# A smaller scratch for dynamic transfers, one more weight page and one more 4 KB buffer, in a two-layer mixer and expert network

## The chip, the cores and the metric

The kernel runs on one core of one Trainium2 chip, in one launch. The metric is the device time of that core in microseconds (us). Of the kernel before there are three timed runs: 2033.0, 2022.24 and 2030.6 us, with a median of 2030.6 us.

## What is computed

The reference is a network of two layers on two sequences of 256 tokens of width 1024, the context and the latent tokens, in float32. Cut to what matters here:

```python
for l in range(2):
    p_lat = dot(x * (1 + sc1) + sh1, w_in[l])            # w_in: 1024 x 3536
    p_ctx = dot(ctx * (1 + mod_c[1]) + mod_c[0], w_in[l])
    y_ctx, y_lat = token_mixers(p_ctx, p_lat, ...)       # attention, RWKV, mLSTM
    x = layer_norm(alpha * x + g1 * dot(y_lat, w_out[l]))
    h2 = x * (1 + sc2) + sh2                             # the same for ctx in layer 0
    f = hierarchical_moe(h2, ...)                        # 32 experts, 2 a token
    x = layer_norm(alpha * x + g2 * f)
```

An expert is `dot(silu(dot(h, w_gate)) * dot(h, w_up), w_down)` with three matrices of 1024 x 512 (or 512 x 1024) in float32, 2 MB each. All 32 experts of a layer get tokens, so each layer reads 192 MB of expert weights.

## The kernel before, in words

**Stages.** A layer has a mixer stage (projections, the three mixers, output projection, norm, router logits) and an expert stage. By the trace, the mixer stage of layer 0 runs from 0 to about 535 us, the experts of layer 0 to about 1075, the mixer stage of layer 1 to about 1510, and the experts of layer 1 with the last norm to the end.

**Pages.** Weights come into a pool named `ring` (line 221) of `NR` = 8 pages of 8 KB a partition, 1 MB each; `rg` (line 272) hands one out. Half an expert matrix fills a page. The same pages also hold the chunks of `w_in`, the modulation weights `w_mod`, `w_out`, the split input of the projections and some intermediates of the mixers. A second pool `hp` (line 239) has `NH` = 12 buffers of 4 KB; `h` and `hr` hand them out, for projected queries and keys, rows spread over the partitions, gathered tokens of the experts (`xe`) and their outputs (`yh`, `yl`).

**Order.** Nearly all loads are issued from SP's queue, one after the other; a load waits there until its page has been let go by its last reader, and everything behind it on SP waits too. The framework sorts the instructions of each engine ahead of time, by priorities (the table `CHOICES['pr']`) and by when it thinks that buffers come free, so the number of buffers enters that order. In the expert stage the matmuls alone are held in the order of the program (`self.pin`, line 1768).

**Expert stage.** `PLAN` (line 37) lists, for each layer, items of one, two, three or four experts, which go through 128 slots of tokens together. `experts` (line 1628) makes the steps of an item: in `first` the tokens go through gate and up, in `second` through down; `moe` (line 1723) weaves the steps of one item with those of the next. `first` goes over the eight row blocks of a matrix and, in each, over all experts of the item: an item of four experts holds four pages at a time and lets go of them together, one of two experts two.

```python
1646:             for (xe, so, runs), ps in zip(blocks, pgu[kind]):
1647:                 for c, m, r in runs:
1648:                     self.mm(ps[c:c + m, :], xe[half][:, j, so + c:so + c + m], wt[r][j], half + j == 0, half + j == 4)
```

`wpart` (line 1698) issues a load; line 1709 is the load into a page. Which expert comes at which rank is known only after the router (`etab`, read by SP). Experts 31 (and 30 in layer 1) are fixed, and their pages are loaded ahead of it (`ahead`, line 1915): in layer 0 four parts into pages and two into 4 KB buffers, in layer 1 seven into pages and the rest into other buffers.

**Scratch.** `Bacc` (line 2012) sets up the program. It reserves, unless told otherwise, 16 KB of each partition as a scratch for dynamic transfers. Sixteen transfers are issued from POOL (the profile's queue q0).

Of the kernel before, what the change touches and what calls it, by code (L numbers as in the profile page):

```python
# [144 lines left out]
        'tks': None,  # L145
        'pr': {'rw_mid': -200}}]}
CFG = dict(CHOICES)
NR, NH, NW, NQ = 8, 12, 15, 8
PB, PC, PE_ = 4, 2, 2
_NP = 69  # L150
_C = {}
# [1868 lines left out]
```

## Time and profile before

| what | value |
|---|---|
| median of three runs | 2030.6 us (2022.24 to 2033.0) |
| the profiled execution's own time | 2033.04 us |
| its span | 2031.2 us |
| mean granted TensorE clock | 0.949 of full speed |
| TensorE (PE) busy | 1800.4 us, 89% of the span |
| VectorE (DVE) / ScalarE (ACT) / GpSimd (POOL) busy | 47% / 25% / 13% |
| read from memory | 523.44 MB, 261 GB/s over the span |

The profile is of one execution. PE is TensorE's matmuls, SPq is the queue of SyncE, from which loads are issued. A view of waits lists who waited, at which line and on which tile, for whom. A view of stretches lists what each engine did between two times, the granted clock and how busy the sixteen transfer engines were.

### The profile page before, as it was taken

What the parts mean: (1) busy time and instruction counts of PE and PEld (TensorE: products, weight loads), DVE (VectorE), ACT (ScalarE), POOL (GpSimd) and SP (SyncE); (2) the same over time, 40 slices, a digit from 0 to 9 for tenths busy, and PEclk for the clock granted to TensorE, in tenths of its full rate; (3) what the DMA queues carried; (4) which work ended last, traced back from release to release, by engine and by line L of the source; (5) the groups of instructions that cost most, each with busy time, mean ns of one, the idle gap of its engine ahead of it and who ended that gap; (6) DMA issues with size and microseconds to landing.
All of it is one profiled execution on the core that took longest, in us unless ns stands there. A gap on an engine that the chain in (4) does not pass through costs nothing. (4 is left out here: it accounts for less than half of the span.)

```text
span 2031.2 us, 29550 instructions
## 1 busy us (share of the span) xinstructions
PE 1800.4 (89%) x11375; PEld 912.1 (45%) x11375; DVE 958.3 (47%) x2133; ACT 508.8 (25%) x1073; POOL 273.5 (13%) x204
## 2 busy tenths in 40 slices
PE   6999999799998899889996899997999988988884
PEld 2777875245533233324434677773453222323221
DVE  2686655567633334334446687744762222222223
ACT  1663413444110010001014654314521010100001
POOL 0000010034311112111221010010220001001001
PEclk9988999999999999999998899988899999999997
DMA  8432335733779998999992233347748979999995
GB/s 282 141 82 58 89 62 217 244 145 104 285 284 382 409 384 327 407 394 396 386 413 87 88 89 95 67 114 251 290 177 350 388 288 415 417 416 409 417 418 227
DMA packets 194224, 532.93 MB, mean 262 GB/s; under 512 B 77824, under 2 KB 108448, under 8 KB 156576
## 3 DMA queue, kind: packets, MB, share of 16 engines
q1 hardware_dynamic: 191936, 526.33, 68.9%
q0 software_dynamic: 992, 2.53, 0.4%
q8 instruction: 92, 1.51, 0.3%
q10 hardware_dynamic: 1152, 2.13, 0.3%
q14 instruction: 52, 0.43, 0.1%
HBM read 523.44 MB, written 7.50 MB: 261 GB/s over the span
## 5 line engine op out<-in xcount | busy, mean ns | idle before, releaser
L283 PE MATMUL ps<-rg,xe 128*32 128x512 f32 (+2 forms) x2280 | 478.0, 614 | 47.3 <-DMA rg<-in_exp_w_up_dram 27.7
L283 PE MATMUL pe<-rg,HT 128*32 128x512 f32 (+2 forms) x1120 | 236.0, 658 | 55.5 <-DMA rg<-in_exp_w_down_dram 44.4
L283 PE MATMUL ps<-rg,wh 128*128 128x512 f32 (+2 forms) x1056 | 260.0, 390 | 5.0 <-ACT wh L473 2.7
L283 PEld LDWEIGHTS ps<-rg,xe 128*32 128x32 f32 (+2 forms) x2280 | 107.8, 123 | 282.6 <-issue 180.3
L1686 DVE TENSOR_TENSOR sc<-pw,bc 128x512 f32<-128x512 f32 x164 | 112.1, 690 | 220.3 <-PE pw L283 218.9
L283 PEld LDWEIGHTS ps<-rg,wh 128*128 128x128 f32 (+1 forms) x1056 | 182.4, 195 | 53.8 <-issue 13.3
L1687 POOL TENSOR_TENSOR acc<-acc,sc 128x512 f32<-128x512 f32 x82 | 106.0, 1293 | 587.5 <-DVE sc L1686 587.5
L283 PEld LDWEIGHTS pe<-rg,HT 128*32 128x32 f32 (+2 forms) x1120 | 66.0, 131 | 220.6 <-issue 122.0
L1676 DVE SCALAR_TENSOR_TENSOR yl<-pe,sw,yh 128x512 fp32r<-128x512 f32 x54 | 40.4, 750 | 237.4 <-ACT yh L1675 234.6
L1675 ACT ACTIVATE yh<-pe,sw 128x512 fp32r<-128x512 f32 x54 | 36.9, 687 | 311.1 <-PE pe L283 288.2
L1652 ACT ACTIVATE H<-ps 128x512 f32<-128x512 f32 x27 | 16.1, 598 | 313.1 <-DVE acc L1687 302.9
L283 PE MATMUL pw<-oh,hi 128*128 128x256 f32 x336 | 90.7, 306 | 1.5 <-DVE oh L1590 1.5
L283 PE MATMUL pw<-yh,ot 128*128 128x512 f32 x164 | 84.2, 513 | 1.8 <-DVE sc L1686 1.5
L283 PE MATMUL pw<-oh,lo 128*128 128x256 f32 x336 | 83.8, 285 | 0.0
L283 PEld LDWEIGHTS pw<-yh,ot 128*128 128x128 f32 x164 | 30.7, 187 | 116.4 <-DVE sc L1686 57.6
L283 PEld LDWEIGHTS pw<-oh,hi 128*128 128x128 f32 x336 | 64.7, 192 | 39.8 <-issue 24.1
L283 PE MATMUL ps<-wh,rg 128*128 128x256 f32 x384 | 77.7, 294 | 0.0
L1622 POOL TENSOR_TENSOR ot<-m,m 128x512 fp32r<-128x512 f32 (+1 forms) x27 | 27.3, 1011 | 328.7 <-PE pw L287 282.5
L1624 DVE SCALAR_TENSOR_TENSOR m<-m,row 128x512 f32<-128x512 f32 (+1 forms) x54 | 28.3, 561 | 91.3 <-POOL ot L1622 91.3
L283 PE MATMUL pw<-yl,ot 128*128 128x512 f32 x164 | 65.7, 400 | 0.7 <-DVE yl L1676 0.5
L1687 DVE TENSOR_TENSOR acc<-acc,sc 128x512 f32<-128x512 f32 x82 | 64.6, 787 | 2.6
L283 PEld LDWEIGHTS pw<-oh,lo 128*128 128x128 f32 x336 | 65.0, 193 | 1.0 <-issue 1.0
(418 smaller groups left out, 2619.9 us busy)
## 6 DMA issues: line engine op xcount, KB each, us to landing
rg<-in_exp_w_up_dram SPq DMA_DIRECT2D x127, 1024.0 KB, 11.2
rg<-in_exp_w_gate_dram SPq DMA_DIRECT2D x126, 1024.0 KB, 10.4
rg<-in_exp_w_down_dram SPq DMA_DIRECT2D x124, 1024.0 KB, 10.6
rg<-in_w_mod_dram SPq DMA_DIRECT2D x40, 1024.0 KB, 7.0
rg<-in_w_in_dram SPq DMA_DIRECT2D x26, 1024.0 KB, 5.5
rg<-in_w_mod_dram SPq DMA_DIRECT2D x16, 512.0 KB, 9.5
rg<-in_w_out_dram SPq DMA_DIRECT2D x8, 1024.0 KB, 8.7
bc<-modd SPq DMA_DIRECT2D x12, 512.0 KB, 5.2
```

Source lines behind the costliest of these rows:

```text
L283: return self.inorder(self.nc.tensor.matmul(out, lhsT, rhs, start=start, stop=stop, skip_group_check=True))
L1622: nc.gpsimd.tensor_tensor(ot, m[0], m[1], ALU.add)
L1624: V.scalar_tensor_tensor(m[k], m[k], 1.0, self.wrow[k][:, :T], ALU.mult, ALU.mult, accum_out=sw[:, k:k + 1])
L1652: nc.scalar.activation(H, pgu[0][b], AF.Silu)
L1675: nc.scalar.activation(yh[:, sl], py[h2], AF.Copy, scale=sw)
L1676: V.scalar_tensor_tensor(yl[:, sl], py[h2], sw, yh[:, sl], ALU.mult, ALU.subtract)
L1686: V.tensor_tensor(tm, ps, self.g2b[0 if t >= 2 else 1][:, sl], ALU.mult)
L1687: (V if hf else nc.gpsimd).tensor_tensor(self.acc[t][:, sl], self.acc[t][:, sl], tm, ALU.add)
```

## The change

```diff
-NR, NH, NW, NQ = 8, 12, 15, 8
+NR, NH, NW, NQ = 9, 13, 15, 8
...
-    nc = bacc.Bacc("TRN2", target_bir_lowering=False, num_devices=1)
+    nc = bacc.Bacc("TRN2", target_bir_lowering=False, num_devices=1, dynamic_dma_scratch_size=4096)
```

The scratch goes from 16 KB of each partition to 4 KB. The 12 KB hold a ninth page of 8 KB in `ring` and a thirteenth buffer of 4 KB in `hp`. No line that computes or loads is changed; what is loaded ahead of the router is listed by name and stays as it was.

## Rows read from the trace of the kernel before

**Rows 1.** The page: TensorE's busy time; the transfer engines' busy tenths in 40 slices.
```profile
PE 1800.4 (89%) x11375; PEld 912.1 (45%) x11375; DVE 958.3 (47%) x2133; ACT 508.8 (25%) x1073; POOL 273.5 (13%) x204
...
DMA  8432335733779998999992233347748979999995
```

**Rows 2.** Stretches, the two mixer stages: length, engines' busy us, clock, transfer share, GB/s.
```profile
0.00:535.00 535.00, 488.46 (x3568) 310.22 (x3572) 322.26 (x750) 223.03 (x495) 75.74 (x48) 0.96 0.47 149
1080.00:1500.00 420.00, 367.36 (x3062) 260.75 (x3063) 268.25 (x599) 185.18 (x414) 52.72 (x43) 0.91 0.43 133
```

**Rows 3.** Waits of TensorE for expert weights: us in total, times, longest us.
```profile
PE pe L283 <- DMA rg<-in_exp_w_down_dram: 44.4, 31, 2.9
PE ps L283 <- DMA rg<-in_exp_w_up_dram: 27.7, 23, 1.5
PE ps L283 <- DMA rg<-in_exp_w_gate_dram: 19.2, 17, 1.5
```

**Rows 4.** Waits of SP's queue, the largest: loads waiting for TensorE's last read.
```profile
SPq L1709 <- PE ps L283: 558.6, 105, 18.6
```

**Rows 5.** Loads of expert weights: count, size, median us to land; range of line 1709.
```profile
rg<-in_exp_w_up_dram SPq DMA_DIRECT2D x127, 1024.0 KB, 11.2
...
DMA to landing us min/median/max: 5.0/10.6/16.3
```

**Rows 6.** Stretches of the expert stages, transfers idle and then busy in turn.
```profile
555.00:572.00 17.00, 17.00 (x75) 10.49 (x75) 1.91 (x10) 4.45 (x8) 0.00 (x0) 1.00 0.08 20
572.00:615.00 43.00, 38.95 (x199) 14.57 (x199) 17.12 (x32) 3.17 (x5) 6.36 (x5) 1.00 0.97 386
615.00:620.00 5.00, 5.00 (x45) 3.60 (x47) 2.17 (x4) 0.42 (x1) 0.00 (x0) 1.00 0.34 77
620.00:709.00 89.00, 71.89 (x449) 21.22 (x441) 28.30 (x51) 5.92 (x10) 12.78 (x10) 0.98 1.02 417
709.00:714.00 5.00, 5.00 (x40) 4.03 (x41) 2.17 (x4) 0.00 (x0) 0.00 (x0) 1.00 0.35 107
714.00:753.00 39.00, 34.62 (x154) 13.26 (x152) 12.48 (x22) 3.76 (x6) 7.46 (x6) 0.91 1.02 417
753.00:793.00 40.00, 40.00 (x268) 17.90 (x264) 19.12 (x37) 3.77 (x6) 6.59 (x6) 1.00 0.79 289
793.00:861.00 68.00, 59.27 (x385) 18.95 (x377) 26.65 (x45) 5.14 (x8) 11.49 (x9) 0.97 1.01 416
861.00:867.00 6.00, 6.00 (x45) 4.37 (x46) 2.17 (x4) 0.60 (x1) 0.00 (x0) 1.00 0.49 171
867.00:920.00 53.00, 47.02 (x209) 13.88 (x206) 18.18 (x37) 4.54 (x7) 7.66 (x6) 0.94 1.02 418
920.00:1055.00 135.00, 135.00 (x618) 53.31 (x617) 61.07 (x105) 12.68 (x20) 28.02 (x22) 1.00 0.99 397
1520.00:1532.00 12.00, 11.91 (x74) 7.28 (x74) 3.61 (x11) 3.58 (x7) 0.00 (x0) 1.00 0.18 48
1532.00:1600.00 68.00, 60.64 (x320) 18.37 (x320) 14.14 (x36) 4.96 (x8) 4.01 (x4) 0.98 1.00 408
1620.00:1660.00 40.00, 34.41 (x145) 13.19 (x146) 6.16 (x15) 4.14 (x7) 0.72 (x1) 0.91 0.60 224
1660.00:1995.00 335.00, 287.77 (x1364) 91.32 (x1364) 85.58 (x179) 27.79 (x44) 32.71 (x30) 0.97 1.02 416
```

**Rows 7.** Waits: TensorE for an expert's scaled output; SP's queue in the mixer stages.
```profile
PE pe L283 <- DVE yl L1676: 3.6, 1, 3.6
...
SPq L453 <- DVE wh L474: 130.4, 11, 34.4
SPq L322 <- DVE pg L1267: 39.4, 2, 38.8
```

**Rows 8.** Queues and issues: the transfers of POOL's queue.
```profile
q0 software_dynamic: 992, 2.53, 0.4%
...
rope<-in_rope_dram POOLq DMA_DIRECT2D x2, 256.0 KB, 4.5
```

## The prediction

> **What bounds the kernel now.** I read the page first. TensorE is busy for 1800.4 of 2031.2 us, and the transfer engines are full in two long runs of slices, the expert stages, and a third to a half busy elsewhere [rows 1]. So there are stages with different limits, and the next view is that of stretches. In the mixer stages TensorE works for 488.5 of 535 us and 367.4 of 420, with the transfers at 0.47 and 0.43 [rows 2]: matmuls and dependences set the pace there, weights don't. In the expert stages it changes hands. The waits of TensorE for expert weights add up to 44.4 + 27.7 + 19.2 = 91.3 us [rows 3]. The waits of SP's queue show the other side: line 1709 stood for 558.6 us, over 105 waits, until TensorE had read a page for the last time [rows 4]. Loads wait for pages and matmuls wait for loads, in turn.
>
> The stretches show the turns [rows 6]. From 555 to 572 us the transfers run at 0.08 while TensorE is busy throughout: all eight pages are held. From 572 to 615 they are full, and TensorE loses 43 - 38.95 = 4.05 us. Such a pair comes seven times. The idle halves start at 555, 615, 709, 753 and 861 in layer 0, at 1520 and 1620 in layer 1. TensorE's idle time in the halves behind them is 4.05, 17.1, 4.4, 8.7, 6.0, 7.4 and 47.2 us, together 95, about the 91.3 of its waits for weights. From 920 to 1055 there is no such loss (135 of 135 us busy): there TensorE is the bound, though the transfers are at 0.99.
>
> **The change part by part.**
>
> *The ninth page.* It adds no instruction and no byte. It lets one more load of 1 MB be issued before the oldest page is let go. While transfers are full that brings nothing by itself: 416 or 417 GB/s is the most that any row shows, at a share of 1.02 [rows 6]. It pays where they stop for want of a page and TensorE later runs short: one load more is then done in the idle half, and the full half behind it is shorter by the time of that load. A load is 1024 KB [rows 5], 1.0486 MB, and at 417 GB/s that is 2.51 us. The gain of a pair is the least of three: this 2.51, the idle time of the transfers in the first half, and TensorE's wait in the second. The transfers' idle time is the length times one less the share: 15.6, 3.3, 3.3, 8.4, 3.1, 9.8 and 16.0 us. All are above 2.51, and so are all seven waits. The upper end is 7 x 2.51 = 17.6 us.
>
> The lower end counts only the four long idle halves (555, 753, 1520, 1620): 4 x 2.51 = 10.0 us. In the three short ones, of 3.1 to 3.3 us, a part of the idle time is the start of a load and no lack of a page. The quickest landing after issue was 5.0 us [rows 5], 2.5 more than the transfer's own 2.5. As loads that follow each other overlap that start, I count the short ones at two thirds: 10.0 + 3 x 1.67 = 15.0 us. Five pairs lie in layer 0, so about 10 us of it come there and 5 in layer 1. The last pair is the surest: from 1660 to 1995 the transfers never pause, so one load more behind them at 1660 moves the end by a load.
>
> By the Trainium skill (SBUF — State Buffer, Summary: rules for kernel authors) a transfer between HBM and SBUF is to be reckoned at about 358 GB/s, the memory's limit, and not at the fabric's 436. A load would then take an estimated 2.93 us, and the seven pairs 20.5 us. The trace disagrees with it: 416 GB/s held for 335 us [rows 6].
>
> *The ninth page in the mixer stages.* It also lets loads of `w_in` and `w_mod` be issued earlier, and the order of SP, DVE and ACT, which the framework works out from the buffers, may shift. The trace of before can't show that order. Bounds: on the good side the idle time of TensorE in these stages, 46.5 and 52.6 us [rows 2], which is mostly dependences, so a tenth, 10 us, is the most that I credit. On the bad side one wait as long as SP's longest here, 38.8 us [rows 7]. I take 0, since the nearest rows, the 88 to 91% busy of TensorE, say that loads are covered. What covers them is matmul work of other heads and mixers; without it the price is that of the rival on SP's order.
>
> *The thirteenth 4 KB buffer.* In the expert stages TensorE waited once for a scaled output that such a buffer holds, 3.6 us [rows 7]. The gain lies between 0 and 3.6, the loss between 0 and the same 38.8 of a shifted order, which is counted once. I take 0.
>
> *The smaller scratch.* Sixteen transfers of POOL, 992 packets and 2.53 MB in 2031 us [rows 8], run there, 0.4% of the engines. No instruction of theirs goes. If they fit, the price is 0; if each waited for the landing of the one before, 16 x 4.5 us [rows 8] = 72 us, were none of it covered. I take 0, the row of 0.4% being the nearest.
>
> **The sum.** Against the profiled execution's own 2033.0 us: 2033.0 - 15.0 = 2018.0. That execution was 2.4 us above the median of 2030.6, which is what the forecast is for: 2015.6, say 2016 us. Half a percent, 10.2 us, is about what a measurement here can tell from no change.
>
> **The rivals.**
>
> *Half of it goes (no change that can be told).* Only some of the pairs pay. Pages are let go in fours or twos, so a ninth page may be idle until three more are free, or the order in the mixers costs some microseconds. For it: the three short pairs, and that items of four experts need four pages at once. Against it: the last pair, where whatever was loaded ahead counts to the end. With two pairs counted and nothing else, 2030.6 - 5 = 2025.6; its range is 2021 to 2033.
>
> *A load gets ahead on SP (slower).* Place: SP's queue in the mixer stages, where loads of pages stand in one line with the small transfers of the RWKV inverse (lines 712, 748, 760, 763), on which RWKV's chain hangs. With a ninth page the order worked out ahead can put a load in front of such a transfer although, on the chip, its page is still held. For it: such waits exist, 34.4 and 38.8 us long [rows 7]. Against: eleven waits of line 453 add up to 130.4 us already, and TensorE still was 88 to 91% busy, and with more pages a load waits less. Price: with a 38.8 us hold and 8 of it covered, 2030.6 - 15 + 31 = 2046.6 us. It decides from a net loss of 25 us on: 15 to eat the gain, 10 for the bound of slower.
>
> *The scratch is too small (slower).* POOL's transfers wait for room. The gain of 15 against a price of up to 72 gives up to 2088 us; with a third of it uncovered, 2040. For it nothing speaks but the size; against it, that the transfers are few and far apart. The Trainium skill (Debugging Trainium Hangs, Descriptor Overflow) says that too many descriptors for the 16 KB carve-out on the Pool queue hang a kernel. No run here shows that.
>
> *More than the pairs.* The mixers gain too, up to the 10 us above, for 2005.6.
>
> **How the numbers follow.** Forecast (2009 to 2020): 0.55. Mixers gain too: 0.05. Half of it goes: 0.27. SP's order: 0.11. Scratch: 0.02. Faster by over 0.5% are the first two, 0.60; within 0.5% 0.27; slower 0.13. The likeliest case and the 'half' case together reach from 2009 to 2033. For the mixers' bounds, 10 us of gain and some loss, the range goes to 2001 below and 2035 above; it leaves out the slower cases and the edges, some 0.16.
>
> **What would show it.** In both layers one load more of ranked experts is issued right behind the router, before TensorE lets go of the first page. TensorE's waits for expert weights fall from 91.3 to about 76 us; the idle halves shrink by 2 to 3 us each; the stretch before the last norm still has transfers at 1.02 and 416 GB/s. The mixer stages keep their lengths within 5 us each. The forecast is wrong if waits for expert weights stay near 91, if a mixer stage grows by over 10 us, or if POOL's transfers land later than now.

## The result, and the profile after

The changed kernel took 2013.4 us in the median of seven runs (2001.3 to 2017.7), the kernel before 2028.5 us in seven beside it. The ratio is 0.9913, with a 95% interval of 0.9893 to 0.9933: 15.1 us faster. The forecast was 15 us, to 2016, in a range of 2009 to 2020. The profiled execution took 2013.38 us, with a span of 2011.5 us, 19.7 less than the span of the profile before; single executions of one kernel lie up to 16 us apart, so the medians decide on the whole and the profile on where it lies.

The waits of TensorE for expert weights, after the change [rows 3]: who waited, on which tile, us in total, times, longest.

```profile
PE pe L283 <- DMA rg<-in_exp_w_down_dram: 36.1, 26, 1.9
PE ps L283 <- DMA rg<-in_exp_w_up_dram: 26.1, 20, 1.5
PE ps L283 <- DMA rg<-in_exp_w_gate_dram: 18.7, 17, 1.5
```

They add up to 80.9 us, 10.4 less. That is only half of what the expert stages lost, so the stretches have to be read. Here are the seven pairs of [rows 6] in the profile after, cut by hand at the same turns of the transfers: length, then busy us of TensorE, of its weight loads, DVE, ACT and POOL, granted clock, share of the transfers, GB/s.

```profile
554.00:571.00 17.00, 17.00 (x77) 10.70 (x77) 1.91 (x10) 4.83 (x8) 0.00 (x0) 1.00 0.21 89
571.00:614.00 43.00, 39.93 (x218) 16.03 (x216) 17.80 (x33) 3.17 (x5) 6.36 (x5) 1.00 0.98 383
614.00:619.00 5.00, 5.00 (x44) 2.96 (x44) 1.48 (x3) 0.80 (x2) 0.02 (x1) 1.00 0.88 297
619.00:704.00 85.00, 71.27 (x437) 22.11 (x430) 28.30 (x51) 5.53 (x9) 12.78 (x10) 0.96 1.02 417
704.00:709.00 5.00, 5.00 (x36) 3.55 (x35) 2.17 (x4) 0.60 (x1) 0.00 (x0) 1.00 0.90 330
709.00:746.00 37.00, 34.42 (x157) 13.54 (x156) 15.09 (x31) 3.17 (x5) 7.66 (x6) 0.95 1.02 418
746.00:786.00 40.00, 40.00 (x284) 17.60 (x286) 16.51 (x29) 3.77 (x6) 6.42 (x5) 1.00 0.84 327
786.00:850.00 64.00, 57.76 (x369) 18.95 (x362) 26.65 (x45) 5.14 (x8) 11.51 (x9) 0.95 1.01 418
850.00:856.00 6.00, 6.00 (x42) 3.52 (x40) 2.17 (x4) 0.60 (x1) 0.00 (x0) 1.00 0.84 304
856.00:906.00 50.00, 44.99 (x206) 13.38 (x204) 18.19 (x37) 4.54 (x7) 7.67 (x6) 1.00 1.02 417
1508.00:1520.00 12.00, 11.91 (x75) 7.17 (x75) 3.25 (x10) 3.58 (x7) 0.00 (x0) 0.99 0.37 128
1520.00:1588.00 68.00, 61.92 (x341) 19.10 (x337) 15.64 (x38) 6.33 (x10) 4.02 (x4) 1.00 1.02 417
1605.00:1645.00 40.00, 34.40 (x141) 13.03 (x139) 6.16 (x15) 4.14 (x7) 0.72 (x1) 0.87 0.64 248
1645.00:1976.00 331.00, 284.38 (x1358) 90.56 (x1354) 85.58 (x179) 27.80 (x44) 32.77 (x30) 0.97 1.02 417
```

Read the idle halves first. The transfers' idle time (length times one less the share) was 15.6, 3.3, 3.3, 8.4, 3.1, 9.8 and 16.0 us; it is now 13.4, 0.6, 0.5, 6.4, 1.0, 7.6 and 14.4. Each is 1.6 to 2.8 us less, 15.6 in all. The bytes (length times GB/s) say the same more sharply: the seven halves moved 1.17, 1.10, 1.12, 1.52, 0.80, 0.96 and 0.96 MB more, 7.6 MB in all, where seven loads are 7.3. So about one load went into each, into the short ones as much as into the long. Then the full halves: they run at 417 or 418 GB/s but for the first (383), and five of the seven are shorter, 85 us for 89, 37 for 39, 64 for 68, 50 for 53, 331 for 335; the first and the one from 1520 keep their 43 and 68 us.

The first sign that the prediction named is there too. Right behind the router SP issues five loads of ranked experts in layer 0, at 543.0 to 547.2 us, where it issued four before, and two in layer 1, where it issued one; the next ones stand until TensorE lets go of a page, at 570.1 and 1517.6 us.

Cut at the first and the last matmul on expert weights, as the timeline has them, the four stages took the times below, in us. The experts of layer 0 so begin at 559.8 us before, some 25 us behind the rough 535 that the words on the kernel before give.

| kernel | pages | mixers 0 | experts 0 | mixers 1 | experts 1 |
|---|---|---|---|---|---|
| before | 8 | 559.8 | 513.1 | 453.2 | 485.4 |
| after | 9 | 559.2 | 499.3 | 455.5 | 477.8 |

Their stretches, before and then after:

```profile
0.00:559.80 559.80, 510.75 (x3726) 325.61 (x3726) 338.99 (x823) 225.54 (x502) 79.09 (x49) 0.95 0.48 155
559.80:1072.90 513.10, 470.92 (x2479) 175.72 (x2477) 198.93 (x366) 44.81 (x71) 84.25 (x66) 0.98 0.95 379
1072.90:1526.10 453.20, 395.01 (x3196) 276.30 (x3196) 294.44 (x686) 192.97 (x428) 64.11 (x48) 0.91 0.43 136
1526.10:2011.40 485.30, 420.60 (x1973) 133.19 (x1973) 111.82 (x239) 41.59 (x67) 39.98 (x37) 0.96 0.96 390
```

```profile
0.00:559.20 559.20, 503.92 (x3726) 322.23 (x3727) 343.38 (x823) 225.86 (x502) 79.22 (x49) 0.97 0.49 157
559.20:1058.40 499.20, 466.66 (x2478) 175.29 (x2476) 198.86 (x366) 44.74 (x71) 84.37 (x66) 0.98 0.96 387
1058.40:1513.90 455.50, 394.87 (x3196) 277.61 (x3194) 292.89 (x686) 192.32 (x428) 65.51 (x48) 0.91 0.44 137
1513.90:1991.70 477.80, 414.45 (x1973) 132.81 (x1973) 111.65 (x239) 41.64 (x67) 40.05 (x37) 0.96 0.96 394
```

The expert stages gave 13.8 and 7.6 us; the mixer stages together lost 1.7. A stage's length moves with the granted clock too: in layer 0's mixers TensorE was busy for 510.8 us at a clock of 0.95 before and for 503.9 at 0.97 after. So for the mixers TensorE's idle time in the stage (its length less TensorE's busy time) is the better measure: in layer 0 it rose from 49.1 to 55.3 us, in layer 1 from 58.2 to 60.6.

### The profile page after: what moved, and what is told of

It is laid out like the page before. It is cut to its first block, busy times and chain, and to the rows that moved or that the text cites. A ratio compares the mean times of both kernels' runs of the same rounds, so it can differ in the third digit from the quotient of the medians.

```text
span 2011.5 us, 29533 instructions
## 1 busy us (share of the span) xinstructions
PE 1783.0 (89%) x11375; PEld 909.2 (45%) x11375; DVE 961.0 (48%) x2133; ACT 508.4 (25%) x1073; POOL 275.2 (14%) x204
## 5 line engine op out<-in xcount | busy, mean ns | idle before, releaser
L283 PE MATMUL pe<-rg,HT 128*32 128x512 f32 (+2 forms) x1120 | 228.7, 638 | 46.8 <-DMA rg<-in_exp_w_down_dram 36.1
L283 PE MATMUL ps<-rg,wh 128*128 128x512 f32 (+2 forms) x1056 | 255.0, 387 | 4.7 <-ACT wh L473 2.4
L283 PEld LDWEIGHTS ps<-rg,wh 128*128 128x128 f32 (+1 forms) x1056 | 181.4, 194 | 53.7 <-issue 13.8
## 6 DMA issues: line engine op xcount, KB each, us to landing
rg<-in_exp_w_up_dram SPq DMA_DIRECT2D x127, 1024.0 KB, 12.2
rg<-in_w_mod_dram SPq DMA_DIRECT2D x16, 512.0 KB, 10.9
bc<-modd SPq DMA_DIRECT2D x12, 512.0 KB, 4.2
```

Of the source, the lines that this page charges most:

```text
L283: return self.inorder(self.nc.tensor.matmul(out, lhsT, rhs, start=start, stop=stop, skip_group_check=True))
```

## Experiments

Each was timed in five rounds with runs of the kernel before on the same chip. The stages of all of them stand in a table at the end of this section.

**The page alone, the buffer alone, the scratch alone.**

```diff
 page alone:    NR, NH, NW, NQ = 9, 12, 15, 8    scratch 4096
 buffer alone:  NR, NH, NW, NQ = 8, 13, 15, 8    scratch 4096
 scratch alone: NR, NH, NW, NQ = 8, 12, 15, 8    scratch 4096
```

> Theory (the ninth page pays in the expert stages): the experts of layer 0 take 499 us and those of layer 1 478 us, within 3 us each, as with the whole change (513.1 and 485.4 before), and the time is 12 to 18 us under the kernel before, whatever the 4 KB buffer does. Rival (the thirteenth 4 KB buffer, or the order that it brings): the page alone gives less than half, under 8 us, and expert stages of over 506 and 482 us.

> Theory: the 4 KB buffer alone changes nothing that can be told: expert stages of 513 and 485 us within 3 us, the time within 5 us of the kernel before. Rival (the buffer carries the gain): 8 us or more under the kernel before.

> The smaller scratch alone, with the buffers as before. Theory: the time is that of the kernel before within 4 us, and POOL's transfers take the same from issue to landing (rope 4.5 us, gw 5.9 us in the median, within 1.5 us). Rival (POOL's transfers wait for room in the smaller scratch): POOL's transfers land later by several us each and the mixer stages grow, 5 us or more in all. Rival (a smaller scratch helps by itself): 5 us or more faster.

The page alone measured 0.9911 (0.9887 to 0.9936), the buffer alone 0.9991 (0.9974 to 1.0008), the scratch alone 1.0002 (0.9986 to 1.0017). With the page the experts took 498.0 and 480.5 us, with the buffer 512.9 and 487.0. So the page carries it; the buffer and the scratch each do nothing that can be told in the time, though the buffer alone already moves 39 of VectorE's 823 instructions in layer 0's mixer stage out of their order. With the scratch alone the instructions of every engine stood in the same order as before (a few matmul records are missing from the traces), and POOL's transfers took the same [rows 8]; from the issues by line, with KB each and median us to landing:

```profile
rope<-in_rope_dram POOLq DMA_DIRECT2D x2, 256.0 KB, 4.4
...
gw<-in_w_in_dram POOLq DMA_DIRECT2D x2, 64.0 KB, 5.8
```

The rival of the scratch is out at 4 KB, for the sixteen transfers of this kernel.

**Where the ninth page works.** A page was taken out of use in one kind of stage: it is handed out, touched by POOL, and read by DVE at the end, so that it can't be let go earlier.

```diff
 held in the experts (nine pages in the mixers, eight in the experts)
+            self.hold = self.rg((2048,))                 # ahead of line 1915
+            nc.gpsimd.memset(self.hold[:, 0:1], 0.0)
...
+        V.tensor_tensor(self.sm([1], 'hd'), self.hold[:, 0:1], self.acc[self.tl[-1]][:, 0:1], ALU.add)   # behind line 1795

 held in the mixers (eight pages in the mixers, nine in the experts)
+            self.hold = self.rg((2048,))                 # behind line 1876
+            nc.gpsimd.memset(self.hold[:, 0:1], 0.0)
...
+            nc.vector.tensor_tensor(self.sm([1], 'hd'), self.hold[:, 0:1], self.Lg[:, len(self.tl) - 1, 0:1], ALU.add)   # ahead of line 1902
```

> The whole change, but one page is held from the loads ahead of the router to the end of the planned items, so that the experts have eight pages again. Theory: the expert stages go back to 513 and 485 us within 4 us, and the time is within 6 us of the kernel before. Rival (the gain comes from the mixer stages, or from the order of the instructions there): still 10 us or more under the kernel before, with expert stages of 499 and 478 us.

> The whole change, but one page is held from the start of a layer to its router logits, so that the mixer stages have eight pages and the experts nine. Theory: the expert stages are those of the whole change, 499 and 478 us within 4 us, and the time is 10 to 20 us under the kernel before. Rival (the ninth page pays in the mixer stages): expert stages of 513 and 485 us and a time within 6 us of the kernel before.

Held in the experts, the kernel was 1.0026 (1.0010 to 1.0042) of the one before: the gain is gone, and 5 us are lost. Held in the mixers it was 0.9893 (0.9868 to 0.9918), with a median of 2003.5 us, 22 us under the kernel before: the gain is there in full, and the time is 2 us better than the 10 to 20 expected. The stretches of the two, cut at the expert matmuls, columns as above, from the mixers of layer 0 on; first with the page held in the experts, then in the mixers:

```profile
0.00:556.50 556.50, 504.17 (x3724) 321.57 (x3727) 343.78 (x823) 225.92 (x502) 79.59 (x50) 0.97 0.49 156
556.50:1068.50 512.00, 471.64 (x2479) 176.27 (x2477) 198.97 (x366) 44.71 (x70) 84.31 (x66) 0.98 0.94 380
1068.50:1527.20 458.70, 395.72 (x3192) 277.29 (x3194) 294.18 (x687) 192.16 (x428) 65.35 (x49) 0.90 0.42 134
1527.20:2016.50 489.30, 425.04 (x1973) 134.08 (x1973) 112.00 (x239) 41.63 (x67) 39.98 (x37) 0.95 0.95 386
```

```profile
0.00:554.70 554.70, 507.41 (x3724) 321.24 (x3727) 343.40 (x824) 225.77 (x502) 79.59 (x50) 0.97 0.49 158
554.70:1053.90 499.20, 466.85 (x2478) 175.44 (x2477) 198.79 (x366) 44.72 (x71) 84.26 (x66) 0.98 0.96 387
1053.90:1505.90 452.00, 388.42 (x3192) 274.81 (x3194) 293.62 (x687) 193.11 (x428) 64.24 (x49) 0.92 0.44 138
1505.90:1979.30 473.40, 413.54 (x1973) 132.58 (x1973) 111.60 (x239) 41.64 (x67) 40.02 (x37) 0.97 0.97 397
```

The experts go back to 512.0 and 489.3 us where the page is held there, and stay at 499.2 and 473.4 where it is held elsewhere (layer 1 misses its expectation twice, by 0.3 us too long and 0.6 too short). The first line of each is the mixer stage of layer 0. At the same clock of 0.97 TensorE is idle for 52.3 us with nine pages there and for 47.3 with eight, so the ninth page seems to cost something in it. The third line is the mixer stage of layer 1, 458.7 and 452.0 us; TensorE's idle time is the same in both, 63.0 and 63.6, and the difference is busy time, at a clock of 0.90 against 0.92, so that these two don't show a cost in layer 1.

**A tenth page.**

```diff
-NR, NH, NW, NQ = 9, 13, 15, 8
+NR, NH, NW, NQ = 10, 12, 15, 8      # scratch 1536 instead of 4096
```

> Ten pages, twelve 4 KB buffers, 1.5 KB of scratch. Theory (each page more moves one load of 2.5 us into every pause of the transfers that is left, no more than the pause): of the pauses left with nine pages three are longer than 2.5 us (one of 14 us ahead of layer 0's first expert, one of 6 us, and in layer 1 one of 8 us and one of 17 us in pieces, four in all) and three are 1.3 to 1.7 us: 4 x 2.5 + 4.5 = 14.5 us less than with nine at most, and two thirds of that, 9 us, at least if short pauses don't pay; the experts take 489 to 493 us in layer 0 and 473 to 475 in layer 1. Rival (the ninth page was enough and the transfers are the bound): within 4 us of the whole change. Rival (scratch of 1.5 KB is too small): POOL's transfers land later and the mixers grow by 10 us or more.

> The changed kernel again, beside the two others on the same chip: 13 to 17 us under the kernel before, expert stages of 499 and 478 us within 2 us.

Ten pages measured 0.9914 (0.9889 to 0.9939), the change beside it 0.9926 (0.9904 to 0.9948). The theory was right in the experts, 490.2 and 473.4 us, and wrong on the whole: the time is that of nine pages. The stretches of the kernel with ten pages show where it went:

```profile
0.00:560.40 560.40, 503.23 (x3724) 321.77 (x3727) 342.32 (x823) 225.66 (x502) 79.34 (x49) 0.97 0.49 158
560.40:1050.50 490.10, 460.50 (x2478) 175.15 (x2476) 198.81 (x366) 44.78 (x71) 84.32 (x66) 0.99 0.97 393
1050.50:1512.20 461.70, 395.98 (x3194) 277.93 (x3194) 298.33 (x686) 192.28 (x428) 65.27 (x48) 0.90 0.43 138
1512.20:1985.60 473.40, 415.39 (x1972) 132.51 (x1973) 111.58 (x239) 41.66 (x67) 40.04 (x37) 0.96 0.97 395
```

The mixer stage of layer 1 takes 461.7 us, against 455.5 with nine pages and 453.2 with eight (this kernel has twelve 4 KB buffers, as the one before). TensorE is idle in it for 65.7 us, against 60.6 and 58.2. One wait there grows with the pages, that of TensorE for DVE's copy at line 810. It isn't listed for layer 1 before; with nine pages and with ten it is:

```profile
PE pw L283 <- DVE PV L810: 3.6, 2, 3.3
```

```profile
PE pw L283 <- DVE PV L810: 7.9, 2, 4.2
```

With nine pages it only takes the place of another one, for ScalarE at line 824, which before was

```profile
PE pw L283 <- ACT T L824: 4.3, 1, 4.3
```

and is 0.2 us after the change; with ten pages the wait at line 810 is some 4 us more than either.

In layer 0 a wait is new, for a small transfer behind RWKV's inverse (line 763). After the change, in the mixer stage of layer 0:

```profile
PE pw L283 <- DMA XX<-dX: 3.4, 2, 3.1
```

It is 3.1 to 3.8 us in each of the six profiled executions with nine or ten pages in the mixers, and isn't there in the six with eight. Before, SP issued this transfer at 139.8 us and TensorE read it first at 147.7, with projection matmuls in between; after the change it was issued at 135.2 and TensorE stood at it until 138.4. No load stands in front of it on SP.

POOL's `rope` and `gw` landed in 4.3 and 5.8 us with 1.5 KB of scratch too.

**Ten pages for the experts, eight for the mixers.** If the page pays in one stage and costs in the other, both can be had. The edit is that of ten pages, and two pages are held in the mixers as above.

> Ten pages, of which two are held from the start of a layer to its router logits, so that the mixer stages have eight pages and the experts ten. Theory (each page more pays in the expert stages; the order with more pages costs some us in the mixer stages): expert stages of 490 and 473 us within 3 us as with ten pages, mixer stages of 555 and 452 us within 5 us as with one page held there, and with 20 us for the end 1990 us, 30 to 38 us under the kernel before. Rival (what ten pages gained in the experts is lost because the transfers run further ahead of the mixers' end, whatever page they use): about 2010 us, mixer stages of 560 us and more, or 460 us and more in layer 1.

> Nine pages with one held in the mixer stages, again, beside the changed kernel on the same chip. Theory: 4 to 10 us under the changed kernel, most of it in the mixer stages (555 and 452 us). Rival (that difference was one of chips and runs): within 4 us of it.

> The changed kernel beside the two others: 13 to 17 us under the kernel before; mixer stages of 553 to 560 and 455 us.

The first measured 0.9803 (0.9785 to 0.9820), 1988.4 us: 38 us under the kernel before and 27 under the change beside it. Its stretches:

```profile
0.00:554.00 554.00, 503.66 (x3725) 320.49 (x3726) 339.66 (x825) 225.34 (x502) 79.36 (x51) 0.97 0.49 159
554.00:1042.40 488.40, 459.28 (x2478) 174.82 (x2476) 198.78 (x366) 44.82 (x71) 84.26 (x66) 0.99 0.98 396
1042.40:1496.90 454.50, 394.92 (x3196) 275.51 (x3194) 292.94 (x688) 192.71 (x428) 64.21 (x50) 0.91 0.44 140
1496.90:1970.00 473.10, 415.66 (x1972) 132.50 (x1972) 111.56 (x239) 41.65 (x67) 39.99 (x37) 0.96 0.97 396
```

The mixers are back at 554.0 and 454.5 us and the experts keep 488.4 and 473.1. TensorE's idle time in the mixers is 50.3 and 59.6 us, with ten pages there it was 57.2 and 65.7. This kernel also sets the order apart from the page: SP issues its 391 loads of expert weights in the order of the kernel before, and VectorE's and ScalarE's instructions stand in their order of before, all but one in the mixers and all in the experts. Yet the experts are 24.7 and 12.3 us shorter. So the gain in the experts comes from the pages and not from a new order.

The kernel with one page held in the mixers measured 0.9904 (0.9887 to 0.9921), the change 0.9945 (0.9928 to 0.9963), a miss of its expectation by some microseconds (11 us under the kernel before, 13 to 17 expected). The intervals of these two don't touch: eight pages instead of nine in the mixers are worth 0.4%, 8 us. In the first comparison, 0.9893 and 0.9926, they overlap. That most of it lies in the mixer stages, as expected, the profiles of these two don't show: 556.7 and 455.9 us with the page held, 553.2 and 457.1 with the change, at a clock of 0.96 and 0.98 in layer 0. TensorE's idle time in layer 0's mixers does show it, 47.4 against 54.1 us.

All stages in us (one profiled execution each; to the tenth they can differ from the rounded stretches), with the ratio of the timed runs:

| kernel | pages in mixers, experts | mixers 0 | experts 0 | mixers 1 | experts 1 | ratio |
|---|---|---|---|---|---|---|
| buffer alone | 8, 8 | 554.2 | 512.9 | 452.7 | 487.0 | 0.9991 |
| scratch alone | 8, 8 | 555.3 | 513.7 | 451.4 | 483.5 | 1.0002 |
| held in the experts | 9, 8 | 556.5 | 512.0 | 458.7 | 489.3 | 1.0026 |
| page alone | 9, 9 | 566.4 | 498.0 | 454.0 | 480.5 | 0.9911 |
| the change again | 9, 9 | 553.4 | 497.4 | 455.6 | 478.0 | 0.9926 |
| the change, third | 9, 9 | 553.2 | 497.4 | 457.1 | 476.2 | 0.9945 |
| held in the mixers | 8, 9 | 554.7 | 499.2 | 452.1 | 473.3 | 0.9893 |
| the same again | 8, 9 | 556.7 | 500.8 | 455.9 | 479.0 | 0.9904 |
| ten pages | 10, 10 | 560.4 | 490.2 | 461.7 | 473.4 | 0.9914 |
| ten, two held in the mixers | 8, 10 | 554.0 | 488.4 | 454.5 | 473.1 | 0.9803 |

Read down the column of experts 0: 512 to 514 us with eight pages, 497 to 501 with nine, 488 to 490 with ten, whatever the rest of the kernel does. The mixer columns scatter by some microseconds from one execution to the next, and only TensorE's idle time tells the kernels apart, and that in layer 0: 47 to 51 us in the six executions with eight pages there, 52 to 55 in the five with nine, 57 with ten. In layer 1 it is 58 to 64 us with eight and 60 to 63 with nine, which is no difference, and 66 with ten.

## Why the prediction was right, and where it was not

**The bound and the mechanism were right.** The stages change hands as read from [rows 6], and the ninth page moves one load into each pause: all seven idle halves shrank, by 1.6 to 2.8 us, with 7.6 MB more moved in them, and the full halves go on at the 417 GB/s of before. Taking the page away from the experts alone took the whole gain away. One reading of the rows was off without an effect: 417 GB/s is not the most that they show, the stretch from 867 has 418 [rows 6].

**The term of the expert stages was too small.** It was put at 15.0 us, 10 in layer 0 and 5 in layer 1. The profile after has 13.8 and 7.6. Over the four profiled executions with eight pages there the means are 512.9 and 486.3 us, over the six with nine 498.7 and 477.5: 14.2 and 8.8, 23 us, above even the upper end of 17.6. In the two profiles of before and after, 21.4 us, most of it can be placed. The three short idle halves moved 3.0 MB more, 7.2 us at 417 GB/s, and not the 5.0 that a count at two thirds gave: the start of a load was no reason for a discount. The four long ones moved 4.6 MB more, 11.0 us for 10.0. What the sum left out are the small pauses in the full halves of layer 1: the half from 1532 ran at 408 GB/s [rows 6] and runs at 417 now, over its 68 us, and the last one went from 416 to 417, together 2.3 us. So 15.0, 2.2, 1.0 and 2.3 make 20.5 us. The rest of the 23 can't be put to a row; single executions scatter by some microseconds.

**The term of the mixers was not 0 but a loss.** It was taken from the row that TensorE is busy there for 88 to 91%, as if that said that loads and order don't matter. That step failed. With nine pages the mixers take about 5 to 8 us more: 7 and 8 by the two comparisons of the change with the kernel whose page is held in the mixers (0.9926 against 0.9893, whose intervals overlap, and 0.9945 against 0.9904), and 5 by the kernel whose page is held in the experts (1.0026), of which some may come from the holding itself. By TensorE's idle time it is some 5 us, all in layer 0. The sum of 15 came out because a gain of some 22 us was put too low by 7 and a loss of some 7 was left out; that they met was luck.

The order worked out ahead is the likely cause, and it isn't shown by itself. With nine or ten pages in the mixers some 100 of VectorE's 823 instructions in layer 0's mixer stage stand out of their order of before; with the page held there it is 40, as with the thirteenth buffer alone, and with ten pages and two held it is one. But holding a page takes back the new order and the earlier loads together. The rival on SP's order, where a load stands in front of a small transfer, is not what the rows show at the largest of the waits that are new in layer 0, 3.4 us for `XX`: the transfer was issued without a load ahead of it, and what went missing is the matmul work that covered it. That is the prediction's own condition, and its price was put too high. The rest of the loss was not taken apart.

**The thirteenth buffer and the scratch** were put at 0, and the runs with each alone have intervals of 0.9974 to 1.0008 and 0.9986 to 1.0017 around it. The wait for a scaled output, 3.6 us [rows 7], that the buffer might have saved was still 3.6 after the change.

**The waits for weights** were to fall to about 76 us; they fell to 80.9. The expectation took a wait and a loss for the same thing. TensorE's busy time fell too, by 4.3 us in the experts of layer 0 and 6.2 in those of layer 1: the down matmuls of 32 columns, which wait for loads one after the other, are shorter by the mean in layer 0, before and after:

```profile
L283 PE MATMUL pe<-rg,HT 128*32 128x512 f32 x384 | 59.4, 653 | 19.1 <-DMA rg<-in_exp_w_down_dram 19.1
```

```profile
L283 PE MATMUL pe<-rg,HT 128*32 128x512 f32 x384 | 55.8, 631 | 10.9 <-DMA rg<-in_exp_w_down_dram 10.9
```

These are from the groups of TensorE between 560 and 1058 us: count, busy us, mean ns, idle time before them. So a part of what weights cost seems to lie inside the matmuls' own times; no run shows that by itself.

## What to carry to other kernels

Where loads wait for pages and matmuls wait for loads in turn, cut the stage into pairs of an idle and a full half: a page more was worth about one load's time for each pause, long or short, as long as a wait followed, and the next page again 9 and 4 us of what was left. Give the page to the stage that has such pairs and to no other: a page more elsewhere can cost, here about a third of the gain, and with ten pages holding two back there gave 2.0% in place of 0.9%. When a sum comes out right, check its terms stage by stage, since two wrong ones can meet in it.

## What was not expected of the hardware

The transfers kept 416 to 418 GB/s with one load more in flight, and the median from issue to landing of the loads of up weights rose from 11.2 to 12.2 us, and to 14.4 with ten pages: a longer queue, at the same rate. POOL's transfers took the same times with 16, 4 and 1.5 KB of scratch (`rope` 4.5, 4.4 and 4.3 us, `gw` 5.9, 5.8 and 5.8), so nothing of the up to 14.5 KB taken was in their way.
